# Squares summed by TensorE, a float32 spread, and written orders in a recurrent decoder step

## The chip, the cores and the metric

The kernel runs on one core of one Trainium2 chip. The metric is the time of one execution in device microseconds (us). Engines are named as the profile names them: PE is TensorE's matmul, PEld its weight load, DVE is VectorE, ACT is ScalarE, POOL is GpSimd, SP is SyncE, which issues the DMAs here.

## What is computed

One layer of a hybrid recurrent decoder is run over a prompt of 1024 positions and over 8 single new tokens, so over 1032 columns in all. The model width is 1024. What matters here of the reference, shortened:

```python
def rmsnorm(x, g):
    y = x32 * lax.rsqrt(jnp.mean(x32 * x32, axis=-1, keepdims=True) + EPS)
    return y * g
...
hn = rmsnorm(x, norm1_g) * (1 + sc1) + sh1
proj = hn @ w_in                          # lru_x 512 | lru_gate 512 | s5_u 512
hs, lru_last = rg_lru(conv(lru_x), ...)   # gates r, i: sigmoid; a = exp(log_a); h = a*h + b
lru_out = hs * gelu(lru_gate)
s5_out = s5_layer(s5_u, ...)              # ends in za * sigmoid(zb), za|zb = gelu(y) @ w_glu
merged = concat([rmsnorm(lru_out, g_lru_out), rmsnorm(s5_out, g_s5_out)])
x32 = x + g1 * (merged @ w_out)
hn2 = rmsnorm(x32, norm2_g) * (1 + sc2) + sh2
ffn = (silu(hn2 @ w_gate) * (hn2 @ w_up)) @ w_down
y = rmsnorm(x32 + g2 * ffn, final_norm_g)
```

## The kernel before

Everything is held with channels on the 128 partitions and the 1032 columns along the free axis. A value that TensorE multiplies is kept as a pair of fp32r tiles, a high part (written by a ScalarE copy, line 96) and a low part (value minus high part, a subtraction through the helper of line 69). A product of two such pairs is three matmuls: high times high, high times low, low times high (lines 142 to 144 for the projections and the GLU, 1302 to 1304 for the output projection, 1478 to 1480 in the feed-forward part). Line 69 is the helper of all element-wise operations of two tensors, line 87 that of the three-operand form, line 126 loads a weight raw through SP into one of two buffers.

The columns are cut in two ways. Up to the GLU they go in 3 chunks of 344 (`CW`). From the output projection on they go in 4 blocks of 258 (`CH`), and blocks 0 and 2 make column half z=0, blocks 1 and 3 column half z=1.

TensorE runs in the order in which the program is written, from the first line to the last. ScalarE does so from the gates to the end of the GLU (the context `ordered`, lines 1115 to 1283). Everything else is ordered by the compiler from dependences and its own estimates.

The stages that matter:

- **Input projection** (before 268 us). `gt_out` (line 1001) takes the result of gate block m out of PSUM: `in_out` (710) multiplies it by the factors of the first norm, and `gt_gelu` (1009) applies the gelu on ScalarE, for blocks 0 to 2 as soon as they are complete, for block 3 later.
- **Recurrence and GLU** (268 to about 349 us). `lru_gates` makes two sigmoids for each of four blocks, `lru_exp` and `lru_tanh` the decay and its square (GpSimd), `lru_scan` the square root, the scan on VectorE and the product of the scan's output with the gated branch into a new tile `lru`. The scan's tiles are stored time-major in eight interleaved steps, so that product reads both operands strided (`steps_first`). `glu` (1164) makes the S5 half's output: a sigmoid on ScalarE and a product on VectorE for each chunk.
- **Norms of the two halves**. `half_square` (1174) squares a block on ScalarE and adds it to the first block's squares on VectorE. `half_rb` (1183) has TensorE sum the result over partitions: `rstd_sums` (175) multiplies it by a column of ones, in four strips of partitions, takes the square root on ScalarE (183) and the reciprocal on VectorE (184), and splits that into a high and a low part (185 to 187). `rstd_spread` (193) multiplies a column of the identity by both parts to spread the factors over all partitions, and ScalarE copies them to SBUF (204). `half_norm` (1192) multiplies by gain and factor and splits.
- **Output projection** (356 to 466 us). It has 32 units, a unit being one of 8 blocks of 128 output channels and one of 4 column blocks. Each unit takes 12 matmuls for the LRU half and 12 for the S5 half (`half_part`, line 1294). Six units run their LRU half ahead; before them, TensorE sums the S5 squares. `out_add` adds the result to the residual, `out_done` (1308) squares and stores it, `rstd_half` (1371) and `norm2_all` (1386) make the second norm of a column half: they normalise it, scale and shift it on ScalarE (1407), form the sums of blocks (`t_blocks`, tile `vn`) and split all of it.
- **Feed-forward part** (from 466.5 us). A product of two 2 by 2 block matrices is made from 7 block products instead of 8. It needs weights in four forms: A (raw), S and T (sums made by GpSimd, line 1446), D. `get` splits a form when it is first asked for, but D at once. `gate_up` (1520) runs 7 products per column half, in the banks X, Z, Y. "The entry" here means its first four passes, from 466.5 to about 535.6 us: gate of half 0, up of half 0, up of half 1, and gate of half 1 with the gate weights loaded a second time (names g0, u0, u0, g0b). The second norm of half 1 is made in the shadow of the first two passes: `rstd_half` hangs on product 1 of the gate pass, `norm2_all` on product 4. From then on the passes take both halves together, with the next pair's weights loaded one pass ahead.

The functions that the change touches and their callers follow.

## Time and profile before

| | before |
|---|---|
| runs | 1193.16 us, median of 3 (1192.72 to 1194.26) |
| the profiled execution | 1192.69 us, of which the span is 1190.9 us |
| granted TensorE clock, mean | 0.954 |
| PE busy | 1093.8 us, 92% of the span |
| PEld busy | 1046.5 us, 88% |
| DVE busy | 853.2 us, 72% |
| ACT busy | 502.4 us, 42% |
| POOL busy | 470.3 us, 39% |
| DMA | 174.93 MB, mean 147 GB/s |
| the chain that ended last | PE 68%, DVE 19%, ACT 5%, issue 3%, POOL 3%, DMA 2% |

The times in all rows count from the start of the span. Busy shares are averages over stages with different limits; the rows further down take stretches one by one. "Idle before" and an arrow name what ended an engine's wait. The granted clock is a share of TensorE's full speed; 1.0 stands for 2.4 GHz, and the lower level is 1.2 GHz.

### The profile page before, as it was taken

To read this page: it belongs to the slowest core of one execution; us is meant where nothing else is said; L and a number is where in the kernel's file an instruction comes from. 1 tells how busy PE (TensorE), PEld (TensorE's weight loads), DVE (VectorE), ACT (ScalarE), POOL (GpSimd) and SP (SyncE) were. 2 spreads that over 40 slices of the span, in tenths; PEclk is the share of its full clock that TensorE was granted. 3 is DMA by queue.
4 is the path that set the end of the run, shared out by engine and by line. 5 is a ranking of instruction groups with operands and counts; after the bars stand their busy time and mean duration, and the time that the engine had idled before them with its cause. 6 is when DMAs were issued, how large, how long until landed. Compare 5 with 4: busy or idle time off the path is not lost.

```text
span 1190.9 us, 21261 instructions
## 1 busy us (share of the span) xinstructions
PE 1093.8 (92%) x8392; PEld 1046.5 (88%) x8392; DVE 853.2 (72%) x1378; ACT 502.4 (42%) x946; POOL 470.3 (39%) x477
## 2 busy tenths in 40 slices
PE   7887988998866999779999999999999999999995
PEld 5776877896856998769999999999999999999995
DVE  6889799833987367876766876687545357778966
ACT  4432323329564144744544544455444431121253
POOL 3397536203400002655555755565433133243012
PEclk8899989999887999889999999999999999999998
DMA  9465446441032232133533442443322876458212
GB/s 344 171 193 176 159 147 176 126 127 39 18 127 71 90 108 89 36 111 140 187 115 126 179 161 102 146 180 145 116 80 72 339 302 258 175 227 275 99 43 101
DMA packets 90628, 174.93 MB, mean 147 GB/s; under 512 B 18720, under 2 KB 54304, under 8 KB 90528
## 3 DMA queue, kind: packets, MB, share of 16 engines
q1 hardware_dynamic: 90528, 173.57, 41.5%
q8 instruction: 66, 1.08, 0.4%
q14 instruction: 34, 0.28, 0.1%
HBM read 126.56 MB, written 46.98 MB: 146 GB/s over the span
## 4 chain that ended last, share of the span: by engine, by line
PE 68%; DVE 19%; ACT 5%; issue 3%; POOL 3%; DMA 2%; SPq 0%; DVEq 0%; POOLq 0%; ACTq 0%
PE X L1478 9%; PE X L1480 9%; PE X L1479 9%; PE Y L1478 5%; PE Y L1480 4%; PE Y L1479 4%; PE o L1302 3%; PE o L1303 3%; PE o L1304 3%; PE Z L1478 2%; PE Z L1480 2%; PE Z L1479 2%; DVE rw L69 1%; DVE xt L69 1%; DVE vt L920 1%
## 5 line engine op out<-in xcount | busy, mean ns | idle before, releaser
L69 POOL TENSOR_TENSOR u<-u,p 128x258 f32<-128x258 f32 x44 | 39.9, 908 | 122.8 <-ACT u L1528 122.8
L142 PE MATMUL in<-hnh,wh_in 128*128 128x344 f32 (+1 forms) x240 | 83.1, 346 | 0.0
L143 PE MATMUL in<-hnl,wh_in 128*128 128x344 f32 (+1 forms) x240 | 79.9, 333 | 0.0
L144 PE MATMUL in<-hnh,wl_in 128*128 128x344 f32 (+1 forms) x240 | 79.7, 332 | 0.0
L69 POOL TENSOR_TENSOR sa_g<-wf_g 128x512 f32<-128x512 f32 x11 | 14.5, 1317 | 158.8 <-PE o L1303 124.8
L69 POOL TENSOR_TENSOR st_d<-wf_d 128x256 f32<-128x256 f32 x32 | 25.8, 825 | 112.4 <-PE X L1480 42.2
L69 DVE TENSOR_TENSOR acc<-X,acc 128x258 f32<-128x258 f32 x128 | 50.0, 420 | 10.3 <-PE X L1480 10.2
L142 PEld LDWEIGHTS in<-hnh,wh_in 128*128 128x128 f32 x240 | 48.0, 200 | 2.9 <-issue 2.9
L143 PEld LDWEIGHTS in<-hnl,wh_in 128*128 128x128 f32 x240 | 47.8, 199 | 0.0
L1528 ACT ACTIVATE u<-X 128x258 f32<-128x258 f32 x88 | 33.3, 382 | 34.5 <-PE X L1480 34.2
L69 DVE TENSOR_TENSOR hs<-v,hs 128x516 fp32r<-128x516 f32 x32 | 46.4, 1466 | 1.8 <-ACT hs L1366 1.7
L144 PEld LDWEIGHTS in<-hnh,wl_in 128*128 128x128 f32 x240 | 47.6, 198 | 0.0
L1303 PE MATMUL o<-ls,wh_s 128*128 128x258 f32 x128 | 37.5, 293 | 5.6 <-DVE ls L69 5.6
L1302 PE MATMUL o<-hs,wh_s 128*128 128x258 f32 x128 | 37.6, 294 | 2.6 <-ACT hs L1201 2.6
L1304 PE MATMUL o<-hs,wl_s 128*128 128x258 f32 x128 | 37.4, 292 | 0.0
L1302 PE MATMUL o<-hl,wh_l 128*128 128x258 f32 x128 | 37.1, 290 | 0.0
L69 POOL TENSOR_TENSOR acc<-acc,rbf 128x388 f32<-128x388 f32 x10 | 11.8, 1211 | 63.4 <-ACT rbf L204 63.4
L1303 PE MATMUL o<-ll,wh_l 128*128 128x258 f32 x128 | 36.8, 288 | 0.0
L1304 PE MATMUL o<-hl,wl_l 128*128 128x258 f32 x128 | 36.8, 287 | 0.0
L69 DVE TENSOR_TENSOR u<-u,u 128x258 f32<-128x258 f32 x42 | 20.3, 484 | 20.1 <-POOL u L69 19.4
L69 DVE TENSOR_TENSOR acc<-Y,acc 128x258 f32<-128x258 f32 x64 | 26.6, 423 | 10.3 <-PE Y L1480 9.6
L69 POOL TENSOR_TENSOR v<-u 128x516 f32<-128x516 f32 x16 | 20.5, 1282 | 34.1 <-DVE u L69 34.1
(1673 smaller groups left out, 4858.7 us busy)
## 6 DMA issues: line engine op xcount, KB each, us to landing
ht<-hs SPq DMA_DIRECT2D x48, 516.0 KB, 3.0
db<-ht SPq DMA_DIRECT2D x48, 516.0 KB, 8.5
ad<-ada SPq DMA_DIRECT2D x48, 512.0 KB, 6.2
wf_g<-w_gu SPq DMA_DIRECT2D x22, 512.0 KB, 3.6
wf_u<-w_gu SPq DMA_DIRECT2D x22, 512.0 KB, 3.3
wf_d<-w_dn SPq DMA_DIRECT2D x16, 512.0 KB, 3.9
wf_in<-w_in SPq DMA_DIRECT2D x10, 512.0 KB, 3.9
x<-xt SPq DMA_DIRECT2D x8, 516.0 KB, 8.0
```

Of the source, the lines that this page charges most:

```text
L69: (e or V).tensor_tensor(out=out, in0=x, in1=y, op=op)
L142: PE.matmul(ps, lhsT=wh, rhs=xh, start=first, stop=False)
L143: PE.matmul(ps, lhsT=wh, rhs=xl, start=False, stop=False)
L144: PE.matmul(ps, lhsT=wl, rhs=xh, start=False, stop=last)
L920: V.tensor_tensor_scan(out=vt[:, ri, q, 8:136], data0=mag8[:, q0 + q:q0 + q + 1].to_broadcast([P, P]), data1=w[ri][:, q], initial=0.0, op0 ...
L1302: PE.matmul(b, lhsT=wh, rhs=xh, start=half == 0 and k == 0, stop=False)
L1303: PE.matmul(b, lhsT=wh, rhs=xl, start=False, stop=False)
L1304: PE.matmul(b, lhsT=wl, rhs=xh, start=False, stop=half == 1 and k == 3)
L1478: PE.matmul(b, lhsT=wh, rhs=xh, start=first and k == 0, stop=False, skip_group_check=True)
L1479: PE.matmul(b, lhsT=wh, rhs=xl, start=False, stop=False, skip_group_check=True)
L1480: PE.matmul(b, lhsT=wl, rhs=xh, start=False, stop=k == nk - 1, skip_group_check=True)
L1528: S.activation(k[name], b[bank], AF.Copy)
```

## The change

- **rstd.** `rstd_sums` and `rstd_half` write the reciprocal to SBUF as float32, without the split into two parts, and the spread is one float32 product with the identity instead of two fp32r products. `rstd_half` sums half the columns in each of four strips.
- **Gate branch.** `in_out` stores the gate blocks with the eight steps first, so that the product with the scan's output reads only one strided operand and is written back into `gt`; the tile `lru` goes. The square of the decay moves from GpSimd to VectorE. The gelu of block 3 and the weights of GLU block 1 move ahead of the gates.
- **Squares.** `half_square` no longer adds; TensorE sums four tiles of squares instead of one. The squares of S5 blocks stand one chunk later, those of the LRU half behind the first output weights. Two output weights' low parts are made by GpSimd. A dummy square root stands at the end of ScalarE's written order.
- **Start of the output projection.** The S5 sums stand behind unit 1 of the six units that run ahead, the spread and the norm of S5 behind unit 3. `out_done` squares each pair of units, the last ones in halves, and the norm of a column half becomes a generator with 12 steps.
- **Entry.** From unit 14 of column half 1 until the end of the fourth pass, ScalarE, VectorE and GpSimd run in written order too. Weight splits and the steps of the second norm are hung on single products of the first two passes; the D form of the up weights is split on request; the weights of the next pair are asked for after the fourth pass instead of ahead of it.

The diff, cut to its core (of `rstd_half` and `norm2_all` only the new lines, the old ones stand in the kernel above):

```diff
-        V.reciprocal(pc[:, 0:q], pc[:, 0:q])
-        r = alloc(f"rs_{name}", 2 * q, F32R)
-        V.tensor_copy(r[:, 0:q], pc[:, 0:q])
-        sub(r[:, q:2 * q], pc[:, 0:q], r[:, 0:q].bitcast(F32))
+        r = alloc(f"rs_{name}", q)
+        V.reciprocal(r, pc[:, 0:q])
...
-                for i in range(2):
-                    PE.matmul(pb[:, j * q:j * q + q], lhsT=identr[:, h * (j0 + j):h * (j0 + j) + 1].to_broadcast([P, P]),
-                              rhs=r[:, i * q:i * q + q], start=i == 0, stop=i == 1)
+                PE.matmul(pb[:, j * q:j * q + q], lhsT=ident[:, h * (j0 + j):h * (j0 + j) + 1].to_broadcast([P, P]),
+                          rhs=r[:, 0:q], start=True, stop=True)
...
+    def by_time(t, lo=0, hi=P):
+
+        return t[:, 0:T].rearrange("p (j k) -> p k j", j=8)[:, lo:hi]
+
+    def in_out(m, c, b, dst, later=False):
 
         cc = slice(c * CW, (c + 1) * CW)
-        mul(dst[:, cc], b[:, 0:CW], rb1[:, cc])
+        if later:
+            n = 8 * (min((c + 1) * kk, P) - c * kk)
+            mul(by_time(dst, c * kk, c * kk + n // 8), kj(b[:, 0:n]), kj(rb1[:, c * CW:c * CW + n]))
+            if n < CW:
+                mul(dst[:, T:TT], b[:, n:CW], rb1[:, T:TT])
+        else:
+            mul(dst[:, cc], b[:, 0:CW], rb1[:, cc])
...
-        in_out(8 + m, c, b, t)
+        in_out(8 + m, c, b, t, True)
...
-        mul(asq, als[m], als[m], G)
+        mul(asq, als[m], als[m])
...
-        lru.append(f(f"lru{m}", TT))
-        mul(steps_first(lru[m]), steps_first(r, True), steps_first(gt[m], True))
-        mul(lru[m][:, T:TT], r[:, T:TT], gt[m][:, T:TT])
+
+        g = gt[m][:, 0:T].rearrange("p (j k) -> p j k", j=8)
+        mul(g, r[:, 0:T].rearrange("p (k j) -> p j k", j=8), g)
+        mul(gt[m][:, T:TT], r[:, T:TT], gt[m][:, T:TT])
...
     def half_square(h, m, lo=0, hi=TT):
 
-        nm, cc, x = h["name"], slice(lo, hi), h["x"][m]
         if m == len(h["sq"]):
-            h["sq"].append(f(f"sq{nm}{m}", TT))
-        S.activation(h["sq"][m][:, cc], x[:, cc], AF.Square)
-        if m:
-            add(h["sq"][0][:, cc], h["sq"][0][:, cc], h["sq"][m][:, cc])
+            h["sq"].append(f(f"sq{h['name']}{m}", TT))
+        S.activation(h["sq"][m][:, lo:hi], h["x"][m][:, lo:hi], AF.Square)
 
     def half_rb(h):
-        r = rstd_sums((h["sq"][0],), 512, h["name"], TT, 4, h["small"])
+        r = rstd_sums(h["sq"], 512, h["name"], TT, 4, h["small"])
...
     w_glu = {0: w_glu0}
+    gt_gelu(3)
+    w_glu[1] = load_w(a["w_glu"][1], "glu1")
     for m in range(4):
         lru_gates(m)
-    w_glu[1] = load_w(a["w_glu"][1], "glu1")
-    gt_gelu(3)
     for m in range(4):
         lru_exp(m)
         lru_tanh(m)
@@ -1261,32 +1260,33 @@
         lru_scan(m)
     for c in range(NC):
         glu(1, w_glu[1], c)
-        if c == 0:
+        if c == 1:
             half_square(hs5, 0)
     w_glu[3] = load_w(a["w_glu"][3], "glu3")
     nc.sync.dma_start(out=o["o_lru"], in_=ol)
     for c in range(NC):
         glu(2, w_glu[2], c)
-        if c == 0:
+        if c == 1:
             half_square(hs5, 1)
-        half_square(hlr, c)
     out_weights(0, 0)
-    half_square(hlr, 3)
+    for m in range(4):
+        half_square(hlr, m)
     for c in range(NC):
         glu(3, w_glu[3], c)
         if c == 0:
+            r_l = half_rb(hlr)
             half_square(hs5, 2)
-            r_l = half_rb(hlr)
+            out_weights(0, 1, G)
         elif c == 1:
             rstd_spread(r_l, "l", hlr["rb"])
         half_square(hs5, 3, c * CW, (c + 1) * CW)
+    S.activation(scr, epst, AF.Sqrt)
     ordered.close()
     half_norm(hlr, 0)
-    out_weights(0, 1)
+    out_weights(1, 0, G)
 
 
...
+    def out_done(z, i, m):
+
+        d, n = m // 2, i // 2
         fl = xz[z][d].rearrange("p b n -> p (b n)")
-        if n == 0:
-            ss[z] = f(f"ss{z}", TT)
-            S.activation(ss[z][:, 0:TT], fl, AF.Square)
-        else:
+        h = slice(2 * CH * (m % 2), 2 * CH * (m % 2) + 2 * CH)
+        if n == 3:
+            if i % 2 == 0:
+                sq3[z] = f(f"sqx{z}_{d}", TT)
+            S.activation(sq3[z][:, h], fl[:, h], AF.Square)
+        elif i % 2:
             q = f(f"sqx{z}_{d}", TT)
             S.activation(q, fl, AF.Square)
-            if n < 3:
+            if n:
                 add(ss[z][:, 0:TT], ss[z][:, 0:TT], q)
             else:
-                sq3[z] = q
+                ss[z] = q
+        if i % 2:
+            nc.sync.dma_start(out=xd[z][d], in_=xz[z][d])
...
-    u0 = ordered_units[0]
-    for m, c in u0[:AHEAD]:
+    for i, (m, c) in enumerate(ordered_units[0][:AHEAD]):
         half_part(m, c, 0)
-    rstd_spread(r_s, "s", hs5["rb"])
-    half_norm(hs5, 0)
-    for mp in range(4):
-        if mp > 1:
-            out_weights(0, mp)
+        if i == 1:
+            r_s = half_rb(hs5)
+        elif i == 3:
+            rstd_spread(r_s, "s", hs5["rb"])
+            half_norm(hs5, 0)
+    out_weights(1, 1)
+    for mp in (2, 3):
+        out_weights(0, mp)
         out_weights(1, mp)
...
+        pc, w = small(f"pc_{name}"), CH // 2
         for t in (ss[z], sq3[z]):
+            for i in range(2):
+                for s in range(4):
+                    PE.matmul(pc[32 * s:32 * s + 32, 0:w], lhsT=ones[:, 0:1].to_broadcast([P, 32]),
+                              rhs=four(t)[:, 2 * i + s // 2, (s % 2) * w:(s % 2) * w + w],
+                              start=t is ss[z] and i == 0, stop=t is sq3[z] and i == 1,
+                              tile_position=(0, 32 * s), skip_group_check=True)
+        S.activation(pc[:, 0:w], pc[:, 0:w], AF.Sqrt, bias=epst, scale=1.0 / D)
+        r = chunk(f"r_{name}", w)
+        V.reciprocal(r, pc[:, 0:w])
         return r
 
...
+    def spread_half(z, r):
+        rb, w = [], CH // 2
         for j in range(2):
             pb = small(f"pb{j}_n2{z}")
+            for s in range(2):
+                PE.matmul(pb[:, s * w:s * w + w], lhsT=ident[:, 32 * (2 * j + s):32 * (2 * j + s) + 1].to_broadcast([P, P]),
+                          rhs=r, start=True, stop=True)
+            rb.append(chunk(f"rb{z}_{j}", CH))
+            S.activation(rb[j], pb[:, 0:CH], AF.Copy)
+        return rb
+
+    def norm2_steps(z, rb):
+
+        vs, shared = [], []
+        for d in range(4):
             u = xz[z][d]
+            for j in range(2):
+                mul(u[:, j:4:2], u[:, j:4:2], rb[j].unsqueeze(1).to_broadcast([P, 2, CH]))
             v = u.rearrange("p (i j) n -> p i (j n)", i=2)
             w_ = 2 * CH - 8 * z
+            if z:
+                t = v[:, :, w_:w_ + 8]
+                mul(t, t, g2n[:, 2 * d:2 * d + 2, 1:9])
+                add(t, t, mod[:, 1, 2 * d:2 * d + 2, 1:9])
             for i in range(2):
                 m = 2 * d + i
                 S.activation(v[:, i, 0:w_], v[:, i, 0:w_], AF.Identity, scale=g2n[:, m, 0:1], bias=mod[:, 1, m, 0:1])
+            yield
+        for d in range(4):
+            u, home = xz[z][d], h_ if d < 2 else f
+            vs.append(four(f(f"vn{z}_{d}", TT)))
+            if z and d % 2:
+                t_blocks(u, vs[d], G)
             if d % 2 == 0:
+                shared.append(home(f"b11_{z}_{d}", TT, F32R))
+            split_first(blks[z][d], u, shared[-1], d % 2)
+            split_two(blks[z][d], u, vs[d], home, f"b{z}_{d}", 0)
+            if d % 2:
+                yield
+        for d in range(4):
+            u, home = xz[z][d], h_ if d < 2 else f
+            if not z or d % 2 == 0:
+                t_blocks(u, vs[d], V)
+            split_two(blks[z][d], u, vs[d], home, f"b{z}_{d}", 1)
+            yield
+        for d in range(4):
+            u, home = xz[z][d], h_ if d < 2 else f
+            split_two(blks[z][d], u, vs[d], home, f"b{z}_{d}", 2)
+            if d % 2:
+                yield
...
+        def make_d():
+            d = f(f"{name}D", 2 * n, F32R)
+            made["D"] = d[:, 0:n], d[:, n:2 * n]
+            split(*made["D"], r1[:, n:2 * n])
+
+        if not lazy:
+            make_d()
 
         def get(which, i):
+            if which == "D" and lazy and "D" not in made:
+                make_d()
...
+    entry = ExitStack()
+    for z in range(2):
+        if z:
+            x_load(1)
+        for i, (m, c) in enumerate(ordered_units[z]):
+            if z or i >= AHEAD:
+                half_part(m, c, 0)
+            half_part(m, c, 1)
+            if z and i == 12:
+                g_w = gu_weights(0)
+                g_w("A", 0)
+            if z and i == 14:
+                entry.enter_context(tc.manual_schedule(engines={ENG.Activation, ENG.DVE, ENG.Pool}))
+            out_add(ubank[m, c], m, c)
+            if i % 2:
+                out_done(z, i // 2, m)
+            if z and i == 0:
+                ra = rstd_half(0, "n2a")
+            if z and i == 2:
+                for _ in norm2_steps(0, spread_half(0, ra)):
+                    pass
+
     ONE = [[(i, z) for i in range(7)] for z in range(2)]
-    g_w = gu_weights(0)
-    u_w = gu_weights(1)
+    norm_b = []
+
+    def rstd_b():
+        norm_b.append(rstd_half(1, "n2b"))
+
+    def spread_b():
+        norm_b.append(norm2_steps(1, spread_half(1, norm_b[0])))
+
+    def go(n):
+        return lambda: pump(norm_b[1:], n)
+
+    u_w = []
+
+    def u_make():
+        u_w.append(gu_weights(1))
+
+    def u_part(which):
+        return lambda: u_w[0](which, 0)
+
     gate_up(u_first, g_w, gate(u_first), order=ONE[0],
-            hooks={(1, 0): [lambda: rb_.append(rstd_half(1, "n2b"))], (4, 0): [lambda: u_w("A", 0), lambda: u_w("T", 0), lambda: norm2_all(1, rb_[0])]})
-    gate_up(u_first, u_w, up(u_first), order=ONE[0])
+            hooks={(0, 0): [u_make, lambda: g_w("S", 0)], (1, 0): [rstd_b, lambda: g_w("T", 0)], (3, 0): [spread_b, go(1)],
+                   (4, 0): [u_part("A"), go(1)], (5, 0): [u_part("D"), go(1)], (6, 0): [u_part("T"), go(1)]})
+    gate_up(u_first, u_w[0], up(u_first), order=ONE[0],
+            hooks={(0, 0): [u_part("S"), go(1)], **{(i, 0): [go(1)] for i in range(1, 6)}})
+    pump(norm_b[1:], 99)
     g_w = gu_weights(0, "b")
-    gate_up(u_first, u_w, up_first, order=ONE[1])
+    gate_up(u_first, u_w[0], up_first, order=ONE[1])
+    gate_up(u_first, g_w, gate_second, order=ONE[1])
+    entry.close()
     nxt = gu_weights(2)
-    gate_up(u_first, g_w, gate_second, order=ONE[1])
```

## Rows read from the trace of the kernel before

**Rows 1.** Stretches, core 0: start:end, span, busy times, PEclk, DMA share, GB/s.
```profile
302.00:331.00 29.00, 25.13 (x146) 24.41 (x144) 29.00 (x35) 12.30 (x16) 10.80 (x4) 0.91 0.06 21
331.00:356.50 25.50, 17.51 (x95) 14.87 (x95) 22.52 (x32) 16.52 (x26) 0.00 (x0) 0.83 0.43 146
356.50:380.50 24.00, 14.86 (x93) 13.94 (x92) 14.52 (x20) 13.11 (x22) 0.00 (x0) 0.71 0.13 44
380.50:466.50 86.00, 86.00 (x705) 85.15 (x705) 53.02 (x95) 24.88 (x37) 7.06 (x4) 0.98 0.27 93
466.50:535.60 69.10, 50.34 (x360) 47.68 (x358) 53.75 (x80) 40.67 (x75) 37.85 (x25) 0.88 0.25 85
```

**Rows 2.** Waits of TensorE, 300 to 381: total us, times, longest.
```profile
PE pc_s L181 <- DVE sqs L69: 5.7, 1, 5.7
PE o L1303 <- DVE ls L69: 5.6, 1, 5.6
...
PE zb L142 <- DVE s5o L69: 3.7, 1, 3.7
PE o L1302 <- ACT hs L1201: 2.6, 1, 2.6
PE pc_l L181 <- DVE sql L69: 1.5, 1, 1.5
```

**Rows 3.** TensorE's timeline, 512 to 513: start, duration, idle before.
```profile
512.86 0.58 PE L1479 MATMUL Z<-b,wh_u0A 128*128 128x258 f32 x1 [6.07 <-DVE b L69]
```

**Rows 4.** ScalarE's timeline, 475 to 477.
```profile
475.45 1.28 ACT L1552 ACT_TABLE_LOAD   x1
476.75 0.42 ACT L1552 ACTIVATE u<-p 128x258 f32<-128x258 f32 x1
```

**Rows 5.** Timelines of ScalarE (ACT) and VectorE (DVE), 268 to 331.
```profile
270.16 0.99 ACT L1133 ACTIVATE r<-r,pk 128x344 f32<-128x344 f32 x2
...
329.93 1.06 ACT L1179 ACTIVATE sqs<-s5o 128x1032 f32<-128x1032 f32 x1 [12.66 <-DVE lru L69]
...
274.91 0.51 DVE L69 TENSOR_TENSOR gt<-in,rb 128x344 f32<-128x344 f32 x1
```

**Rows 6.** Tiles lru, up, r, ll: count, minimum/median/maximum ns, first and last start.
```profile
L69 DVE TENSOR_TENSOR lru<-r,gt x8: 149/1074/2261, 317.8 to 329.8; 128x1024 f32<-128x1024 f32 x4, 128x8 f32<-128x8 f32 x4
...
L69 DVE TENSOR_TENSOR up<-in,rb x8: 159/732/771, 68.9 to 97.9; 128x344 f32<-128x344 f32 x4, 128x336 f32<-128x336 f32 x2, 128x8 f32<-128x8 f32 x2
...
L87 DVE SCALAR_TENSOR_TENSOR r<-asq,r x4: 1217/2077/2931, 293.7 to 303.7; 128x1032 f32<-128x1032 f32 x4
...
L69 DVE TENSOR_TENSOR ll<-lru,hl x8: 689/691/692, 348.3 to 381.6; 128x516 fp32r<-128x516 f32 x8
```

**Rows 7.** VectorE's timeline at 480; its groups, 466.5 to 535.6; tile xz.
```profile
480.24 1.23 DVE L69 TENSOR_TENSOR wl_u0A<-wf_u,wh_u0A 128x1024 fp32r<-128x1024 f32 x1 [1.22 <-ACT wh_u0A L96]
...
L69 DVE TENSOR_TENSOR b<-vn,b 128x516 fp32r<-128x516 f32 x8 | 8.9, 1152 | 0.0
...
L1407 ACT ACTIVATE xz<-xz,mod,g2n x16: 797/806/821, 432.9 to 492.5; 128x516 f32<-128x516 f32 x8, 128x508 f32<-128x508 f32 x8
```

**Rows 8.** Chain of waits, 275 to 290 and 58 to 64.
```profile
281.65 1.74 PE r L1132 x6
...
60.65 0.90 PE pb_n L202 x6
```

**Rows 9.** TensorE's timeline, 349 to 357.
```profile
356.48 0.58 PE L1302 MATMUL o<-hl,wh_l 128*128 128x258 f32 x1
```

**Rows 10.** Tile pc_l.
```profile
L184 DVE RECIPROCAL pc_l<-pc_l x1: 1769/1769/1769, 340.0 to 340.0; 128x258 f32<-128x258 f32 x1
L186 DVE CAST rs_l<-pc_l x1: 428/428/428, 341.8 to 341.8; 128x258 fp32r<-128x258 f32 x1
```

**Rows 11.** ScalarE's timeline, 326 to 360.
```profile
348.74 1.05 ACT L96 ACTIVATE wh_l<-wf_l 128x1024 fp32r<-128x1024 f32 x1
351.23 0.49 ACT L1179 ACTIVATE sqs<-s5o 128x344 f32<-128x344 f32 x1 [1.45 <-DVE s5o L69]
```

More of the change, by code (lines that the diff above doesn't have):

```diff
@@ L1117, in body @@
     l0 = par("l0").rearrange("p (m b) -> p m b", m=4)
-    gates, als, s5o, lru = [], [], [], []
-    def steps_first(t, by_time=False):
-        if by_time:
-            return t[:, 0:T].rearrange("p (k j) -> p j k", j=8)
-        return t[:, 0:T].rearrange("p (j k) -> p j k", j=8)
+    gates, als, s5o = [], [], []
     def lru_gates(m):
@@ L1371, in rstd_half, with split_blocks @@
+    def split_blocks(blk, u, v, home, name, shared, half):
+        split_first(blk, u, shared, half)
+        for i in range(3):
+            split_two(blk, u, v, home, name, i)
     def rstd_half(z, name):
-        pc = small(f"pc_{name}")
+        pc, w = small(f"pc_{name}"), CH // 2
         for t in (ss[z], sq3[z]):
-            for j in range(2):
-                for i in range(2):
-                    PE.matmul(pc[64 * j:64 * j + 64, 0:CH], lhsT=ones[:, 0:1].to_broadcast([P, 64]),
-                              rhs=four(t)[:, 2 * i + j], start=t is ss[z] and i == 0, stop=t is sq3[z] and i == 1,
-                              tile_position=(0, 64 * j), skip_group_check=True)
@@ L1379, in rstd_half @@
-        S.activation(pc[:, 0:CH], pc[:, 0:CH], AF.Sqrt, bias=epst, scale=1.0 / D)
-        V.reciprocal(pc[:, 0:CH], pc[:, 0:CH])
-        r = [chunk(f"r{i}_{name}", CH, F32R) for i in range(2)]
-        V.tensor_copy(r[0], pc[:, 0:CH])
-        sub(r[1], pc[:, 0:CH], r[0].bitcast(F32))
-        return r
-    def norm2_all(z, r):
-        rb = wp.tile([P, 2 * CH], F32, tag="wl", name="rb_a") if z == 0 else f("rb_b", 2 * CH)
+            for i in range(2):
[4 more added lines that the diff above has]
+                              tile_position=(0, 32 * s), skip_group_check=True)
@@ L1453, in weights_of @@
         src = {"A": r0, "S": sa, "T": sb}
-        d = f(f"{name}D", 2 * n, F32R)
-        made = {"D": (d[:, 0:n], d[:, n:2 * n])}
-        split(*made["D"], r1[:, n:2 * n])
+        made = {}
+        def make_d():
[4 more added lines that the diff above has]
+            make_d()
         def get(which, i):
+            if which == "D" and lazy and "D" not in made:
+                make_d()
             if which not in made:
@@ L1491, in gu_weights @@
         r = [load_raw(a["w_gu"][2 * p_ + i, j], f"{name}_{i}") for i in range(2)]
-        return weights_of(*r, 512, name, n in (1, 2 * NP - 1))
+        return weights_of(*r, 512, name, n in (1, 2 * NP - 1), n == 1)
     def dn_weights(n):
```

58 lines of the change are left out of this document (11 added, 47 removed).

## The prediction

> **What bounds the kernel now.** I read the stages first [rows 1]. From 380.5 to 466.5 us, and again in the feed-forward part behind 536, TensorE is busy without a gap at a granted clock near 1.0: there only fewer matmuls would help. What can be won lies in three stretches ahead of them: 302 to 331, 331 to 380.5 and 466.5 to 535.6, which hold 3.9, 17.1 and 18.8 us of TensorE idle at a granted clock of 0.71 to 0.91, so a part of the busy time there runs at 1.2 instead of 2.4 GHz. Second, what TensorE waits for in them [rows 2]: 3.7 us for VectorE's product of a GLU block, 1.5 and 5.7 for the summed squares of the two halves, 2.6 and 5.6 for the split, normed S5 half. The longest wait of the entry to gate and up is 6.1 us for the last split blocks of the second column half [rows 3]. The change touches all of these.
>
> The profiled execution took 1192.69 us (span 1190.9 plus 1.8), 0.5 below the 1193.16 of the runs; the sum is made against 1192.69. A difference of 0.2% is 2.4 us, about what a measurement can tell from no change.
>
> **Recurrence and GLU, 268 to 331.** The gelu of gate block 3 moves ahead of the gates, behind the other gelus, so its own table load falls away: -1.28, the price of another load [rows 4]. But it now stands first in ScalarE's order and waits for VectorE's evacuation of that block, which before came only at 274.9, while the gates began at 270.2 [rows 5]; left there, the gates start some 5 us later and the first GLU sigmoid some 3 later. Between -1.3 and +3.3 I take 0. The gate's evacuation into eight blocks costs 0.73 instead of 0.51 us [rows 5, 6], 12 times, 2.7 us, beside TensorE's projections ahead of 268: nothing; without that cover 2.7. In return the product with the scan's output has one strided operand less: it takes 2.26 us [rows 6]; contiguous, 1.23 (the size of [rows 7], first row). I take 1.7, the middle, since one strided operand stays: four times 0.55, -2.2, bounds 0 and -4.1, in a stretch where VectorE is busy 29.0 of 29 us [rows 1]. The squares of the decay go from GpSimd to VectorE: +4 x 1.23 there, but the four products behind them, 1.22 alone and up to 2.93 beside GpSimd [rows 6], come back to 1.22: even. ScalarE stood 12.7 us in front of the square of S5 block 1, waiting for VectorE [rows 5], and the sigmoids behind it held TensorE's banks; one sigmoid later it holds less. Of the 3.7 us wait I count -3, bounds -4 and 0.
>
> **Sums by TensorE, 331 to 356.** Eight VectorE adds go; the wait of 1.5 at the first sums goes with them. TensorE pays: a float32 product of 344 columns, two records, takes 1.74/3 = 0.58 us [rows 8], so 258 columns take 0.43. Four groups instead of one: +1.3 for each half. The spread takes four such products, 1.74, instead of eight records in about 1.2 (six take 0.90 [rows 8]): +0.5. With the wait: +0.3.
>
> **Start of the output projection.** Before, TensorE stood 5.7 us in front of the S5 sums and only then, at 356.5, began the LRU products [rows 2, 9]. Now two units (24 matmuls, 2.9 us at 86.00/705 = 0.122 each [rows 1]) come first and cover it: -5.5, if the split LRU half is there; sums and spread +1.8: -3.7 (if not covered, +1.8). Behind it the S5 chain: sqrt without its table load, a reciprocal of 1.77 [rows 10], no cast and no subtraction (0.43 [rows 10]), spread after unit 3 instead of after six units. From the first LRU product: 2.9 + 1.7 sums + 2.9 (units 2 and 3 cover sqrt and reciprocal) + 1.7 spread = 9.2; copy, norm, high part, low part 2.4 for the first of four blocks, 1.4 for each further one: 15.8. TensorE has LRU work until 12.1 and uses the blocks one by one, so about 2.5 of wait remain of 8.2 [rows 2]: -5.7. But half of the 8.2 was VectorE's order, chosen by the compiler, which ran other norms ahead of the low parts; it may do so again. I take -4, bounds 0 and -8.2. Splitting two weights' low parts on GpSimd frees VectorE of 2 x 1.23 and is counted at nothing: their users come 10 us later. The norm of column half 0 has sums of 129 columns, four strips at once: -0.9, spread +0.3, TensorE-bound: -0.6.
>
> **Entry to gate and up.** Here three engines get the written order, and it decides. I walk it from TensorE's first gate product (466.5 before). Products are 12 matmuls, 1.46. Second half's sums at 2.9, sqrt behind two table loads (silu, then sqrt, 1.28 each [rows 4]), reciprocal done at 9.3, spread, factors in SBUF at 10.8. Then hooks 3 to 6 of the gate pass each have ScalarE make a weight's high part, VectorE its low part, VectorE two products of the norm, ScalarE two scale-and-bias operations. Each engine goes on only in this order, so the four are one chain: high 1.0 [rows 11], low 1.2 [rows 7], products 1.2 (the low part's size), scale-and-bias 2 x 0.72 (0.81 each [rows 7], overlapping), silu 0.3 (0.42 [rows 4], overlapping), hand-overs 0.1: 5.2 a hook. First step without weights but with the third table load: 4.3; then A 5.2, D (half the columns) 4.3, T 5.0, a copy 0.3: 19.1, to about 30. Only there stands the high part of the up weights' second set, for which TensorE, done with the two products before it at 20.2, waits 11 us. Splits fill 30 to 47; TensorE ends the first column half at 42 and has the second half's T blocks at 46.8: before, 46.4 (512.86 [rows 3]): nothing won. Seven products less two: 54.2. The last pass (10.1) makes its three weight sets only when it comes to them: A behind the last copy, S behind a silu, T behind a copy, each 1.0 + 1.2 and 0.6 to 1.0 ahead of it: 8.7 of waits. End at 73.0 against 69.1 [rows 1]: **+3.9**. Best, if the four hooks overlapped: TensorE's busy 50.3 [rows 1] and those 8.7 give 59: -10. Worst: VectorE's split products cost 1.15 us in the mean here [rows 7], 0.69 alone [rows 6]; with that 0.46 more on some 20 of the chain's VectorE instructions: +9 on top, +13.
>
> Weights 2, loaded and split ahead of the last pass before, now stand behind the written order; SP loads them once the second copy's first split frees a buffer, ten microseconds ahead of the end, and GpSimd has their sums to make behind its last add. If ScalarE made their first high part only after the last silu, TensorE would wait 0.4 + 1.05 + 1.23 = 2.7. But at the end of ScalarE's present written order work from behind it came first: a weight's high part at 348.74, the last square of the order at 351.23 [rows 11]. So I take 0, and 2.7 for the bound. The other moved loads (GLU block 1, the output weights, gate's first weights at unit 12 of 16) go out earlier on SP, under TensorE's 86 busy microseconds [rows 1]; a store of the residual per finished pair of blocks is beside that too. Without that cover they would cost no more than the same 2.7.
>
> On the three loads: a load takes 1.28, and the silu behind it starts 0.02 later [rows 4]. The Trainium skill ("ScalarE: Activation LUTs", What ACT_TABLE_LOAD costs) gives 2.66 us per switch, with a drain. By that the two added switches cost 2.8 more and the entry is +6.7; the row shows no drain, so the sum stays.
>
> **Opening and end.** The first spread: +0.5 on TensorE, which is on the chain there [rows 8]. The last one, of fewer columns, loses a cast and a subtraction on the chain, each at most the 0.43 of [rows 10]; at about half of that, -0.5. Together 0.
>
> **Sum.** 0 - 3 + 0.3 - 2.2 (the strided products: the stretch is VectorE's; half of it stands in the 3 already, so -1.1) gives -3.8; -3.7 - 4 - 0.6 gives -8.3; +3.9. Total -8.2, from 1192.69 to 1184.5, on the runs' level **1185 us**.
>
> **Rivals.** (1) The entry does overlap: the four hooks lie only a product of 1.46 apart, and TensorE's 18.8 us of idle [rows 1] leave room; against it stands the chain above, in which each link needs the one before. Entry -10: 1171. (2) The order costs more: VectorE and GpSimd collide in the chain. For it: the product of 1.22 that took 2.93 beside GpSimd [rows 6] and the 1.15 for 0.69. At +13 the sum is +1, and with the gelu's +3.3, which is the same in-order wait, +4: 1197. It decides from an entry of +12. The Trainium skill ("SBUF — State Buffer", SBUF: two separate sides) says that a GpSimd operation and a VectorE operation with two SBUF inputs exclude each other for the whole instruction; the 2.93 agrees. (3) VectorE's chosen order keeps the low parts late and the square waits: the middle gives only -4, with the entry 0: 1193.
>
> **Chances.** Forecast 0.5, (1) 0.2, (2) 0.16, (3) 0.14. Faster by over 0.2%: 0.5 + 0.2 = 0.70; within: 0.14; slower: 0.16. Range: the forecast with its bounds (the stretch to 380 from about -17 to 0) is 1177 to 1194; to take in (1) and (2) with little to spare: 1169 to 1197.
>
> **What would show it.** Right: no wait for the S5 sums; LRU products from about 350 instead of 356.5; a wait of 8 to 12 us for the high part of up's S weights; in the last pass three waits of 2 to 3 us for weights; three table loads in the entry. Wrong: if that long wait is missing, (1); if the gates start past 275 or the entry lasts over 80 us, (2); if the S5 low parts come 20 us behind the first LRU product, (3).

## The result: slower by 0.9%, all of it lost in the entry

The changed kernel took 1202.64 us (median of 4 runs, 1202.05 to 1204.17), the kernel before 1192.94 beside it: ratio 1.009, 95% interval 1.0062 to 1.0118. The forecast was 1185. The profiled execution took 1202.40 (span 1200.3). I set the two profiles side by side at TensorE's own milestones, since TensorE runs one written order in both:

| TensorE's product, start in us | before | after | stretch up to it |
|---|---|---|---|
| first gate product of the recurrence | 267.7 | 266.7 | -1.1 |
| first LRU product of the output projection | 356.5 | 347.2 | -8.2 |
| first gate product of the entry | 466.65 | 455.27 | -2.1 |
| first product of the next weights (end of the entry) | 535.60 | 544.30 | +20.1 |
| end of the span | 1190.9 | 1200.3 | +0.7 |

So the front won 11.4 us in this profile, where 12.1 were forecast, and the entry, forecast at +3.9 with a bound of +13, lost 20.1. The first row of the table varies by itself: in the eight profiles whose front is that of the changed kernel, the recurrence begins between 266.7 and 270.0 us. From there to the entry these take 188.6 to 189.1 us, and the kernel before 198.9, so without the opening the front is worth 10 us. The stretches of after, which answer to [rows 1]:

```profile
302.00:331.00 29.00, 27.00 (x172) 26.51 (x176) 28.06 (x31) 16.16 (x22) 3.66 (x4) 1.00 0.12 39
347.20:370.00 22.80, 16.60 (x126) 13.68 (x125) 19.93 (x27) 13.65 (x24) 3.29 (x1) 0.90 0.31 104
455.20:544.30 89.10, 55.80 (x379) 51.96 (x378) 51.84 (x74) 42.68 (x76) 31.21 (x25) 0.79 0.19 67
```

The last row is the entry: 33.3 us of TensorE idle instead of 18.8, and 55.8 busy instead of 50.3 at a granted clock of 0.79 instead of 0.88. TensorE's waits in it (454 to 545 us):

```profile
PE X L1504 <- ACT wh_u0S L96: 10.9, 1, 10.9
PE X L1504 <- ACT p L1554: 5.8, 1, 5.8
PE X L1504 <- ACT wh_g0bS L96: 5.5, 1, 5.5
PE pb_n L1404 <- DVE r_n2b L1396: 1.9, 1, 1.9
PE X L1504 <- ACT wh_g0bA L96: 1.4, 1, 1.4
PE X L1504 <- ACT wh_g0bT L96: 1.4, 1, 1.4
```

The first is the forecast wait for the high part of up's S weights (11 us). The chain of waits shows one hook of it, link by link as the prediction walked it: high part, low part, two products, scale-and-bias.

```profile
471.34 0.95 ACT wh_u0A L96
...
472.32 1.23 DVE wl_u0A L69
473.54 0.62 DVE xz L69
...
474.18 0.71 DVE xz L69
...
474.92 0.78 ACT xz L1425
...
476.33 0.40 ACT u L1578
```

The second wait is for a copy that takes 0.37 us. ScalarE's timeline shows where it stood: behind all splits of the second half and a D split that waited for VectorE.

```profile
508.17 0.63 ACT L96 ACTIVATE g0bD<-wf_g0b 128x512 fp32r<-128x512 f32 x1 [2.07 <-DVE b L69]
508.71 0.37 ACT L1554 ACTIVATE p<-X 128x258 f32<-128x258 f32 x1
```

The third is in the last pass. SP could issue the second half of weights 2 only when the A split of the pass had freed its buffer. The compiler had put the D split of weights 2 (g1D) and a first split of the hidden blocks (hb) among the instructions written by hand, ahead of the pass's own add (p), silu (sg) and S split. Timelines of SP, ScalarE and VectorE:

```profile
510.63 10.39 SPq L126 DMA_DIRECT2D wf_g<-w_gu  x2
...
523.89 0.63 ACT L96 ACTIVATE g1D<-wf_g 128x512 fp32r<-128x512 f32 x1 [1.32 <-DMA wf_g<-w_gu]
...
527.62 0.42 ACT L1591 ACTIVATE sg<-p 128x258 f32<-128x258 f32 x1 [2.78 <-DVE p L69]
527.94 1.04 ACT L96 ACTIVATE wh_g0bS<-sa_g0b 128x1024 fp32r<-128x1024 f32 x1
...
524.56 1.28 DVE L69 TENSOR_TENSOR g1D<-wf_g,g1D 128x512 fp32r<-128x512 f32 x1 [3.94 <-ACT g1D L96]
525.77 1.48 DVE L69 TENSOR_TENSOR hb<-u,hb 128x258 fp32r<-128x258 f32 x1
527.17 0.41 DVE L69 TENSOR_TENSOR p<-Z,p 128x258 f32<-128x258 f32 x1
```

### The profile page after: what moved, and what is told of

Same layout as the page of the kernel before. It is cut to its first block, busy times and chain, and to the rows that moved or that the text cites. A ratio compares the mean times of both kernels' runs of the same rounds, so it can differ in the third digit from the quotient of the medians.

```text
span 1200.3 us, 21427 instructions
## 1 busy us (share of the span) xinstructions
PE 1099.2 (92%) x8480; PEld 1047.2 (87%) x8480; DVE 839.8 (70%) x1360; ACT 505.3 (42%) x950; POOL 452.5 (38%) x475
## 4 chain that ended last, share of the span: by engine, by line
PE 67%; DVE 19%; ACT 6%; issue 4%; POOL 2%; DMA 2%; SPq 1%; DVEq 0%; ACTq 0%; POOLq 0%
PE X L1504 9%; PE X L1506 9%; PE X L1505 9%; PE Y L1505 5%; PE Y L1504 5%; PE Y L1506 5%; PE Z L1504 2%; PE Z L1506 2%; PE Z L1505 2%; PE o L1303 2%; PE o L1302 2%; PE o L1304 2%; DVE rw L69 1%; DVE xt L69 1%; DVE vt L927 1%
## 5 line engine op out<-in xcount | busy, mean ns | idle before, releaser
L69 DVE TENSOR_TENSOR u<-Y,u 128x258 f32<-128x258 f32 x44 | 18.6, 423 | 26.5 <-PE Y L1506 26.4
L87 DVE SCALAR_TENSOR_TENSOR xz<-o,mod,xz 128x258 f32<-128x258 f32 (+1 forms) x32 | 15.2, 479 | 31.1 <-PE o L1304 27.5
```

Of the source, the lines that this page charges most:

```text
L69: (e or V).tensor_tensor(out=out, in0=x, in1=y, op=op)
L87: V.scalar_tensor_tensor(out=out, in0=x, scalar=s, in1=y, op0=op0, op1=op1)
```

## The experiments

The theory is that the three engines' written order makes the entry's loss; the rivals are named with each run. "Entry" is the profiled time from the first gate product to the first product of weights 2. The first gate product itself came between 455.3 and 459.2 us in the eight kernels with the same front, so entries are compared within a profile. Differences in time of under 2 us are not resolved: most runs of one kernel spread over 2 to 6 us.

| run | edit | us, median (lowest to highest) | entry, us |
|---|---|---|---|
| before, beside these | | 1191 to 1194 (1188.3 to 1196.7) | 69.0 |
| after | | 1202.64 (1202.05 to 1204.17) | 89.0 |
| e1_free | after, no written order at the entry | 1179.52 (1177.75 to 1179.81) | 64.8 |
| e2_oldentry | after, entry as before | 1175.80 (1173.30 to 1178.62) | 61.8 |
| e3_close | after, written order ends behind weights 2 | 1201.02 (1200.66 to 1205.42) | 83.6 |
| e4_ahead | after, last pass's weights ahead | 1193.99 (1191.02 to 1196.72) | 79.1 |
| e9_act | after, ScalarE's order alone | 1195.06 (1191.47 to 1199.69) | 79.3 |
| e10_dve | after, VectorE's order alone | 1184.97 (1183.68 to 1189.46) | 70.1 |
| e14_unlink | e4, splits ahead of the norm's steps | 1191.79 (1189.52 to 1195.09) | 78.6 |
| e5_gelu | e2, gelu behind the gates | 1174.41 (1173.83 to 1177.54) | 61.4 |
| e6_gtold | e2, gate blocks stored as before | 1177.35 (1175.52 to 1181.57) | 60.7 |
| e7_sqv | e2, squares added on VectorE | 1182.91 (1180.01 to 1184.74) | 62.3 |
| e12_gls | e2, S5 low parts on GpSimd | 1175.46 (1174.79 to 1179.64) | 59.7 |
| e8_perd | e2, norm's steps pair by pair | 1176.93 (1176.15 to 1180.33) | 62.6 |
| e11_rstd | e2, factors made as before | 1176.01 (1174.67 to 1181.66) | 61.5 |
| e13_whole | e2, last square in one piece | 1179.81 (1175.55 to 1181.86) | 66.4 |
| e18_three | e8, e11 and e13 together | 1183.17 (1182.27 to 1186.88) | 68.6 |
| e17_best | e5, last pass's weights asked for ahead | 1175.80 (1175.11 to 1177.63) | 64.0 |

### Is it the written order?

**e1_free.**

```diff
-            if z and i == 14:
-                entry.enter_context(tc.manual_schedule(engines={ENG.Activation, ENG.DVE, ENG.Pool}))
```

> The changed kernel without the written order at the entry; hooks, splits and everything ahead of the entry stay. Theory (the in-order chain of the three engines makes the entry's +20): the wait of 10.9 us for the high part of up's S weights goes and the entry takes 65 to 72 us instead of 89, so 1179 to 1186 us. Rival (the places of the weights and of the norm's steps cost it, not the queues): the entry stays above 80 us and the time above 1193.

It took 1179.5, ratio 0.9889 (0.9862 to 0.9916), with the 10.9 us wait gone. The written order costs 1202.6 - 1179.5 = 23.1 us; hooks and weights that stay where they were cost nothing like it. Its entry:

```profile
456.60:521.50 64.90, 51.59 (x379) 48.78 (x379) 52.57 (x71) 40.60 (x75) 32.17 (x25) 0.87 0.20 68
```

**e2_oldentry.** The entry's code of the kernel before, with the new norm's steps all at product 4:

```diff
...
+    gate_up(u_first, g_w, gate(u_first), order=ONE[0],
+            hooks={(1, 0): [rstd_b], (4, 0): [u_part("A"), u_part("T"), norm_now]})
...
```

> Everything ahead of the entry as changed, the entry's hooks, weights and free order as before. Theory (the front wins 11.4 us and the entry gives back 20): TensorE's first gate product stays near 455 and the entry takes 69 us, so about 1181.5 us. Rival (what is won ahead of the entry is lost in it whatever its order, since the norm of the second half has a floor of its own): the entry takes 75 us or more, 1188 or above.

It took 1175.8, ratio 0.9861 (0.9824 to 0.9898), under both figures: the entry took 61.8, not 69. Nothing won in front is given back, and the entry itself had become shorter, which I had not forecast (below). The hooks' new places, in free order, are no gain either: e1 takes 3.7 us more than e2, with ranges that overlap.

```profile
456.50:518.30 61.80, 48.51 (x378) 46.31 (x377) 53.26 (x72) 40.75 (x73) 32.27 (x25) 0.92 0.25 84
```

Against it the 27.3 us of the changed kernel's entry part in two: 20.0 of idle (33.3 against 13.3) and 7.3 of the same matmuls (378 or 379 recorded) taking longer (55.8 against 48.5) at a clock of 0.79 instead of 0.92.

**e9_act and e10_dve** keep the written order for one engine:

```diff
-                entry.enter_context(tc.manual_schedule(engines={ENG.Activation, ENG.DVE, ENG.Pool}))
+                entry.enter_context(tc.manual_schedule(engines={ENG.Activation}))
```

> The changed kernel with the written order at the entry for ScalarE alone; VectorE and GpSimd ordered by the compiler. Theory (ScalarE's order carries the chain: high part, scale-and-bias, next high part): the entry keeps more than half of the 24 us between the free order and the written one, 1190 to 1200. Rival (VectorE's order is what holds the low parts and products in line; ScalarE alone would run ahead of it): 1180 to 1186.

> The changed kernel with the written order at the entry for VectorE alone; ScalarE and GpSimd ordered by the compiler. With all three it took 1202.6, with ScalarE alone 1195.1, with none 1179.5. Theory (each order holds up by itself, and the chain goes through both engines): 1188 to 1197. Rival (VectorE's order does harm only together with ScalarE's): 1180 to 1184.

ScalarE's order alone costs 15.5 us over the free one, as its theory had it, and VectorE's alone 5.5, which lies between the two figures of its forecast. The sum, 21, is near the 23.1 of all three; GpSimd's order was not run alone. Why ScalarE's is the dearer is not settled: of TensorE's waits in the entry of e9, 6.5 us are two waits for ScalarE's copies out of banks, and some 16 are waits for weights.

### Which link of it?

**e3_close and e4_ahead.**

```diff
-    entry.close()
     nxt = gu_weights(2)
+    entry.close()
```

> The changed kernel with the end of the written order one line later, behind the loads and sums of weights 2, so that their D split and the first splits of the hidden blocks can't stand among the last pass. Theory (the 5.5 us wait for the S weights of the last pass is the D split of weights 2 standing in front of the pass's own add and silu, waiting for its load): that wait falls to 1.5 us or less, and with it the products at the lower clock behind it; -4 to -7 us, 1195.5 to 1198.5. Rival (the wait is the split of S itself, made on request): 1202 within 1.5.

```diff
-    gate_up(u_first, u_w[0], up_first, order=ONE[1])
-    gate_up(u_first, g_w, gate_second, order=ONE[1])
+    gate_up(u_first, u_w[0], up_first, order=ONE[1],
+            hooks={(2, 1): [lambda: g_w("A", 0)], (4, 1): [lambda: g_w("S", 0)]})
+    gate_up(u_first, g_w, gate_second, order=ONE[1], hooks={(2, 1): [lambda: g_w("T", 0)]})
```

> The changed kernel with the last pass's A, S and T weights split two products ahead (hooks of the pass before and of the last one) instead of on request. Theory (each on-request split costs TensorE 1.4 + 0.8 us): the three pairs of waits, 1.4 + 0.8, 1.0 and 1.4 + 0.8, go: -5 us, 1197 to 1198; the stall on the D split of weights 2 may stay. Rival (the splits only trade places with copies and silus that TensorE waits for next): within 2 us of 1202.6.

In e3 the wait for the S weights fell from 5.5 to 2.0 and the entry by 5.4, as the theory says; but the time fell by 1.6 only, which is the rival's figure. The splits that were pushed back are missing next: TensorE waits 2.9 us for the low part of the S form of weights 2, and the first product of the weights behind them (u1) came 23.3 us after the end of the entry instead of 20.5 (564.62 - 541.36 against 564.78 - 544.30), and this profile's front ran 2.5 later. In e4 all the last pass's waits but 3.6 us went, the stall on weights 2 among them: -8.6, more than expected. What was left, 79.1, still holds the 10.9 and the 5.8 us wait.

**e14_unlink** takes the hooks' chain apart, inside the written order:

```diff
-(3, 0): [spread_b, go(1)], (4, 0): [u_part("A"), go(1)], (5, 0): [u_part("D"), go(1)], (6, 0): [u_part("T"), go(1)]
+(3, 0): [spread_b, u_part("A")], (4, 0): [u_part("D"), u_part("T")], (5, 0): [u_part("S"), go(1)], (6, 0): [go(2)]
...
```

> The kernel with the written order and the last pass's weights split ahead (1194.0), and in it the splits of up's A, D, T and S weights hung on products 3 to 5, ahead of the norm's steps, instead of one between each two of them. Theory (high part, low part, products, scale-and-bias of a hook form one chain, and four of them in a row hold up the S weights): the 10.9 us wait for the S weights falls below 2 us, the second half's blocks come some 8 us earlier, 1184 to 1188. Rival (the written order costs whatever the hooks hold, through the buffers and the copies behind the splits): 1191 or more.

The rival holds: 1191.8, 2.2 below e4. The wait for the S weights is gone, and in its place stands one of 9.5 us, at the same product: the copy that empties its bank is queued behind the scale-and-bias of the norm. TensorE's and ScalarE's timelines:

```profile
484.60 0.58 PE L1504 MATMUL X<-b,wh_u0S 128*128 128x258 f32 x1 [9.49 <-ACT p L1554]
...
482.18 0.81 ACT L1425 ACTIVATE xz<-xz,mod,g2n 128x508 f32<-128x508 f32 x1 [0.24 <-DVE xz L69]
483.47 0.81 ACT L1425 ACTIVATE xz<-xz,mod,g2n 128x508 f32<-128x508 f32 x1 [0.48 <-DVE xz L69]
484.19 0.36 ACT L1554 ACTIVATE p<-X 128x258 f32<-128x258 f32 x1
```

So it is not this one chain: a norm that waits for VectorE, written ahead of copies that TensorE waits for, held those up in both places that were tried; in e1, in free order, the longest wait for such a copy is 1.2 us.

### What made the front faster?

**e5_gelu, e6_gtold, e7_sqv and e12_gls** undo or add one thing in the front of e2:

```diff
-    gt_gelu(3)
-    w_glu[1] = load_w(a["w_glu"][1], "glu1")
     for m in range(4):
         lru_gates(m)
+    w_glu[1] = load_w(a["w_glu"][1], "glu1")
+    gt_gelu(3)
```

> The kernel with the old entry (1175.8), and in it the gelu of gate block 3 and the weights of GLU block 1 behind the gates again. Theory (ScalarE held the gates until 276.2 instead of 270.2 because the gelu stands first in its order; the table load that this saves is only part of that, and the first exp comes 2.2 us later after the gates' first product): 1 to 2.5 us faster, 1173.3 to 1174.8. Rival (the gates' delay is made up, since VectorE bounds the scans behind it): within 1 us of 1175.8.

```diff
-        in_out(8 + m, c, b, t, True)
+        in_out(8 + m, c, b, t)
...
-        mul(g, r[:, 0:T].rearrange("p (k j) -> p j k", j=8), g)
+        mul(lru[m][:, 0:T].rearrange("p (j k) -> p j k", j=8), r[:, 0:T].rearrange("p (k j) -> p j k", j=8),
+            gt[m][:, 0:T].rearrange("p (k j) -> p j k", j=8))
```

> The kernel with the old entry (1175.8), and in it the gate blocks stored and multiplied as before: both operands of the product with the scan's output strided, a tile of its own for the result. Theory (one strided operand costs as much as two: the product took 2.15 to 2.26 us in the changed kernel and 2.26 before): within 1 us of 1175.8. Rival (the prediction's saving of 0.55 us on each of four products in a stretch bound by VectorE): 1177 to 1178.

```diff
         S.activation(h["sq"][m][:, lo:hi], h["x"][m][:, lo:hi], AF.Square)
+        if m:
+            add(h["sq"][0][:, lo:hi], h["sq"][0][:, lo:hi], h["sq"][m][:, lo:hi])
...
-        r = rstd_sums(h["sq"], 512, h["name"], TT, 4, h["small"])
+        r = rstd_sums((h["sq"][0],), 512, h["name"], TT, 4, h["small"])
```

> The kernel with the old entry (1175.8), and in it the squares of each half added on VectorE as before, so that TensorE sums one tile instead of four. Theory (nearly ten us of VectorE adds stand in the stretch that VectorE bounds, and the sums of both halves wait for them): +4 to +8 us, 1180 to 1184. Rival (the adds lie beside other waits and TensorE's three more groups cost the same): within 1.5 us.

```diff
-            half_norm(hs5, 0)
+            half_norm(hs5, 0, G)
```

> The kernel with the old entry (1175.8), and in it the low parts of the S5 half's first norm made by GpSimd instead of VectorE. Theory (the 5.6 us that TensorE still waits for the first of them is VectorE's order, which has low parts of the LRU half ahead; GpSimd is idle there): the wait falls to 3 us or less and the run by 2 to 4 us, 1172 to 1174. Rival (GpSimd's subtraction of 128x516 takes so long, and slows VectorE's norms beside it, that the later blocks are waited for instead): within 1.5 us, or slower.

The squares count: with VectorE's adds back, at the squares' new places, the run takes 7.1 us longer, and TensorE stands at the first sums, which [rows 2] had at 1.5:

```profile
340.07 1.09 PE L181 MATMUL pc_l<-sql,ones 128*32 128x258 f32 x8 [8.39 <-DVE sql L69]
```

The storing of the gate blocks does not make the product shorter. The product's row in the changed kernel answers to the first of [rows 6]; e6, with both operands strided, has 2.0 to 2.3 us for the same:

```profile
L69 DVE TENSOR_TENSOR gt<-r,gt x8: 176/1172/2235, 318.9 to 332.3; 128x1024 f32<-128x1024 f32 x4, 128x8 f32<-128x8 f32 x4
```

One strided operand costs as much as two. It steps 32 bytes (eight float32). The Trainium skill ("SBUF — State Buffer", Door 1: The DMA port swizzle (why `[64,N]` ≈ `[32,N]`)) says that each access that crosses to another line of 16 bytes pays; the row agrees, 2.2 against the 1.23 of a contiguous product of that size.

The 1.5 us of e6 (its rival's figure) and the 1.4 of e5 (its theory's) are within the spread of the times. The profiles tell more: from the first gate product of the recurrence to that of the entry the eight kernels with the changed front take 188.6 to 189.1 us. With the gelu behind the gates e5 takes 186.1 and e17, which has the same front, 185.8; the first exp comes 23.1 us behind the gates' first product instead of 25. So the gelu's new place cost some 2.5 us. In e6 the stretch is 191.6: VectorE, in the compiler's order, makes the low part of a GLU weight behind all four products instead of ahead of the last two, and TensorE waits 5.7 us for it instead of 1.4. Whether the storing brings that order about is not shown.

In e12 GpSimd's subtractions took 1.65 us each in the median for VectorE's 0.68: one wait of 5.6 became four of 4.4 in all, and the time stayed, as the rival had it.

### Why is the entry in free order 7 us shorter?

**e8_perd, e11_rstd, e13_whole, e18_three.** e8 writes norm, sums of blocks and all splits of a pair of blocks into one loop, e11 puts back the old bodies of `rstd_half` and of the spread, e13 is

```diff
-            if i % 2 == 0:
-                sq3[z] = f(f"sqx{z}_{d}", TT)
-            S.activation(sq3[z][:, h], fl[:, h], AF.Square)
+            if i % 2:
+                sq3[z] = f(f"sqx{z}_{d}", TT)
+                S.activation(sq3[z][:, 0:TT], fl, AF.Square)
```

and e18 is the three of them.

> The kernel with the old entry (1175.8), and in it the second norm's steps for each of the four pairs of blocks in one go (norm, sums of blocks, all splits), as before, instead of all norms first, then the splits form by form. Theory (the form-by-form order is why the free entry takes 62 us and not 69, since each product needs one form of all blocks): the entry goes back to 66 to 69 us, 1180 to 1183. Rival (the gain is that of the earlier factors, by the float32 spread and sums of 129 columns): within 2 us of 1175.8.

> The kernel with the old entry (1175.8), and in it the factors of the second norm made as before: sums of 258 columns in two strips, reciprocal in PSUM, a cast and a subtraction, spread by two fp32r products. Theory (the free entry takes 62 us instead of 69 because the factors are there 12 us after the first gate product instead of 18): they come 16 to 18 us behind it again, the entry takes 66 to 69 us and the run 1180 to 1183. Rival (the factors come early because the last squares are made in halves, or something else of the front): within 2 us of 1175.8.

> The kernel with the old entry (1175.8), and in it the last pair of blocks squared in one piece behind its last unit, as before, instead of in halves. Theory (the free entry takes 62 us instead of 69 because ScalarE, not held by the whole last square, makes the D split of gate's first weights some 13 us earlier, so their buffer comes free and SP loads up's first weights 2 us ahead of the first gate product instead of 3.4 behind it): the load goes out behind the first gate product again and the entry takes 66 to 70 us, 1180 to 1184. Rival (not that either: the form of the norm's products, or where the blocks lie): within 2 us of 1175.8.

> The kernel with the old entry (1175.8), and in it all three of the second norm's new forms undone at once: the last square whole, the factors by 258 columns with cast and subtraction, the steps for each pair of blocks in one go. Theory (the 7 us between the free entries, 62 and 69, are these three together, of which the whole square alone gave 4.6): the factors come 17 to 18 us behind the first gate product and the entry takes 68 to 70 us, 1182 to 1185. Rival (the whole square is all that counts, the rest is hidden): 66 to 67 us, 1179 to 1181.

My first two answers were wrong: norm order and factors each change nothing alone. The square in one piece brings back 4.6 of the 7.2, the three together 6.8 (68.6 against 69.0). The timelines of ScalarE, SP and TensorE in e13 show what stands behind the last square: the D split of gate's weights, and with it the load of up's weights, which waits for the buffer that the split frees and leaves 3.4 us behind the first gate product (459.86 - 456.44), as in the kernel before (470.02 - 466.65); and the S split of gate's weights, for which TensorE waits:

```profile
457.48 1.07 ACT L1316 ACTIVATE sqx<-xz 128x1032 f32<-128x1032 f32 x1 [7.92 <-DVE xz L69]
458.45 0.61 ACT L96 ACTIVATE g0D<-wf_g 128x512 fp32r<-128x512 f32 x1
...
460.83 1.05 ACT L96 ACTIVATE wh_g0S<-sa_g 128x1024 fp32r<-128x1024 f32 x1
...
459.86 0.81 SPq L126 DMA_DIRECT2D wf_u<-w_gu  x2
...
461.93 0.39 PE L1504 MATMUL X<-b,wh_g0S 128*128 128x258 f32 x1 [1.43 <-ACT wh_g0S L96]
```

The kernel before, D split and load:

```profile
468.60 0.61 ACT L96 ACTIVATE g0D<-wf_g 128x512 fp32r<-128x512 f32 x1
...
470.02 0.81 SPq L126 DMA_DIRECT2D wf_u<-w_gu  x2
```

In e2, with halves, both splits ran before the second half, and the load left SP 1.95 us ahead of the first gate product (456.50):

```profile
453.14 0.61 ACT L96 ACTIVATE g0D<-wf_g 128x512 fp32r<-128x512 f32 x1
453.67 1.05 ACT L96 ACTIVATE wh_g0S<-sa_g 128x1024 fp32r<-128x1024 f32 x1
...
454.55 0.81 SPq L126 DMA_DIRECT2D wf_u<-w_gu  x2
```

That the late load costs anything is not shown: TensorE's wait for a part of up's weights is not longer in e13 (0.8 us for the low part of S, 1.6 in e2). For gate's S split it waits 1.4 us (high part) and 0.8 (low part) in e13, 1.5 and 1.5 in the kernel before and in e18, and not at all in e2, e8 and e11. In sum the entry of e13 has 1.3 us more idle than that of e2 (14.6 against 13.3), and its matmuls take 3.3 us longer (51.8 against 48.5); how much of this follows from the S split is open.

**e17_best** asks for the last pass's weights ahead, as e4 does, in free order.

> The kernel with the old entry and the gelu behind the gates (1174.4), and in it the last pass's weights asked for two products ahead, in free order. Theory (2.6 us are left of waits for the low part of the last pass's T weights): 1 to 3 us faster, 1171.5 to 1173.5. Rival (the compiler places the splits by its own times whatever the program says): within 1 us of 1174.4.

No gain: 1175.8 is 1.4 above e5, within the spread, and the wait for the T weights' low part is 3.3 us. The lowest of all that ran is e5 (ratio 0.9851, 0.9832 to 0.987); e2, e11, e12 and e17 lie within 1.6 us of it and can't be told from it. These are 15 to 19 us ahead of the kernel before and 27 to 28 ahead of the changed one.

## Why the prediction was wrong

- **The front** was near as a sum, partly by luck, since its terms cancel. Up to the first LRU product -7.5 was forecast and -8.2 measured, without the opening's 1.1. The saving on the strided products (-2.2, half of it counted) isn't there. The gelu, put at 0 between -1.3 and +3.3, cost some 2.5 (e5, e17): the gates began at 276.2. A wait of 5.0 us for a sigmoid that empties a GLU bank, which [rows 2] leaves out, fell to 1.5. The step "Eight VectorE adds go" counted TensorE's wait of 1.5 alone; at the squares' new places the adds are worth 7.1 (e7). Behind the first LRU product -4.6 was forecast, -2.1 came: of the 8.2 us of S5 waits 5.6 stayed, in VectorE's order, as the bound allowed. The first low part of S5 began 19.6 us behind the first LRU product, the sign of rival (3).
- **The entry, first part: right.** "TensorE ... waits 11 us" for up's S weights: 10.9. The high part was forecast at about 30 us behind the first gate product and began at 32.2 (487.49).
- **The entry, the step that failed: "Products are 12 matmuls, 1.46".** I let TensorE run on at its upper clock between waits that I had myself forecast at 11 and 8.7 us. The entry's 28 products at 1.46 make 40.9 us. In the changed kernel TensorE was busy 55.8 us there, some 2 of it the norm's sums and spread, at a granted clock of 0.79. Its idle was in sum nearly as forecast: 33.3 us, where the 73.0 of the walk leave about 30. So by my estimate some 13 of the 16 us by which the entry missed the walk (89.0 against 73.0) are matmuls at the lower clock. [rows 1] had the same products and sums at 50.3 us, at 0.88, with 18.8 idle. So the walk set some 11 us more idle, which came, against some 7 us less of busy time, for which the change gives no reason; 5.5 more came. (The 7.3 us against e2 are less than 13, since e2's entry ran at 0.92 and not at 1.) The second half's S product, with its T blocks, was due at 46.8 and began at 53.9. Part of that is the copy behind the splits: my walk held TensorE for blocks and weights only, not for banks that ScalarE empties in the same queue.
- **"So I take 0, and 2.7 for the bound" failed the other way round.** Work from behind the written order did come forward, as [rows 11] let me argue; I took that for a gain. In an in-order queue it stood ahead of the last pass's own silu, and waited for a load: 5.5 us of wait. The last pass took 26.3 us (544.3 - 518.0) where 18.8 were forecast; 2.2 of the difference are waits (10.9 against 8.7), the rest the matmuls' clock.
- **The range** reached to 1197 by rival (2), in which the written order costs more; that is what happened, and both its signs came (gates past 275, an entry over 80 us), but its mechanism, collisions of VectorE and GpSimd, does not make the loss. There are some: from 499.2 to 506.6 us, beside GpSimd's sums for g0b, four VectorE operations ahead of the second half's T blocks took 6.0 us, where such ones take 2.2 by themselves. In all, though, VectorE was busy 51.84 us in the entry, against 53.75 before [rows 1] and 53.26 in e2. What was added are queues and the clock.
- **The table loads** took 1.28 each, as the sum had it; where the Trainium skill ("ScalarE: Activation LUTs", What ACT_TABLE_LOAD costs) has 2.66, this case's rows decide again.

## What to carry to other kernels

An order written out by hand for all engines is worth what its author knew of every queue in it; before trusting it, run the same hooks in free order (here 23 us better). In a written order put the short copies that empty a matmul engine's banks ahead of anything that waits for a third engine, and look at what the compiler slips in between. When waits are forecast for TensorE, price the matmuls behind them at the lower clock, too.

## What the runs showed that I had not expected

One square cut into halves, on an engine that is 42% busy, shortened the entry by 4.6 us; two weight splits that had stood behind it came some 5 to 7 us earlier. And of two strided operands, making one contiguous saved nothing: 2.2 us either way.
